# The sums of squares of q and k one head at a time, and the first S5 input products one tile later, in a two-layer hybrid trunk

## The chip, the core and the metric

The kernel runs on one core of one Trainium2 chip. The metric is the device time of one execution in microseconds (us): the median of three runs. Where time inside an execution is spoken of, it is counted from the first instruction of one profiled execution. PE is TensorE, DVE is VectorE, ACT is ScalarE, POOL is GpSimd, and SP is the engine that issues the transfers.

## What is computed

Two layers. Each is a SwiGLU block (1024 to 2 x 2816 and back, half a step), a mixing of the tokens, and a second SwiGLU block. A sequence is 16 learned tokens and 256 given ones, 272 in all. In the mixing one input projection feeds four groups of 512 channels, and one output projection takes their results back:

```
A: RG-LRU       conv over 4 tokens, h = a*h + b, times a GeLU gate
B: DeltaNet     q, k, v = silu(conv4(u)); q, k divided by their norms, sqrt(sum(x*x)+eps), per head
                S = S*exp(g) + k (beta*(v - ...))^T, done in chunks; 4 heads of 128
C: Mamba-2      conv over 4 tokens, chunked scan with a decay per head
D: S5           x -> complex diagonal state (64 per 16 channels) -> y; gelu; a half GLU
```

The sums of squares that the change moves are those of group B's norms: for each of 4 heads of q and 4 of k, the sum over 128 channels for each token. The S5 input products are those that bring group D's channels to its complex state, in four parts.

## The kernel before

**Tiles and precision.** x lies in SBUF as two halves, `xh` and `xl`, whose sum is x. A weight tile of 128 x 1024 comes by a transfer into `raw` (three buffers) and is split in `ahead` into `hi` (L215, on ScalarE) and `lo` (L217, on VectorE), with four buffers each (`SPLITS`). One tile of the input projection is 24 matmuls (`mm3`, L232 to L234: hi times xh, hi times xl, lo times xh, for 8 blocks of channels) into a PSUM bank `g`; there are four such banks. All other products use four banks `m`. The split of a tile is asked for three tiles ahead, and waits until the tile that last used its `hi` and `lo` buffers has been multiplied.

**What follows a tile.** A tile of q, k, v or of C's convolved channels goes through `conv` (a scaled copy on ScalarE, L540 or L542, and three steps on VectorE, L545) and `silu2` (tanh on ScalarE, L551, and a product on VectorE, L552). Its `g` bank is free once L545 has read it.

**Sums of squares.** `b_sums` (steps `ks` and `qs` with the head's number) squares a head on GpSimd (L580) and sums over channels with three matmuls of one column each (L240, in `token_sums`), into one `m` bank that is held from the first head of k until `b_norms` (step `bn`). A float matmul gives two records in the trace, so a head gives six.

**S5.** `d_in` (step `di`, part 0 to 3) is 8 small matmuls (L1179, 68 columns), four products on VectorE (L1184), two sums on GpSimd (L1185), two scans (L1194), four products (L1184) and two sums on GpSimd into the state `dz` (L1185). `d_out` (step `do`) is 12 small matmuls: L1213 on the input, L1215 on `dz`. ScalarE then copies the result out and SP writes and re-reads it (L1219, L1221). There is one state, so a part must be through `d_out` before the next part writes it. Steps `da` (L1229 and a GeLU, L862 to L865, on VectorE and ScalarE) and `ds` (L1236, ScalarE: the rounded half `dU`) follow, and `dg` is the half GLU: two weight tiles, each of 2 x 12 matmuls on `dU`, which need the four channels' `dU` and two `g` banks.

**Tokens' scalars and decays.** `token_scalars` (step `tk`) transposes (L475) and runs some 40 small VectorE operations (L476 to L491). `decay` (steps `R`, `be`) fills rows on ScalarE (L501), sums them on PE into three `m` banks one after the other (L517; L519 to L521; L523 to L525) and takes the exponential of each on ScalarE (L528), which needs a table load.

**What sets the order.** `STEPS_TEXT` (L81) is a hand-written list of steps, the same for both layers; `mixing` walks it and issues each step's work. A scheduler then fixes, before anything runs, one order of instructions for each engine, from that list and from the dependences. On the chip each engine takes its instructions in that order. So a step that is moved in the list can change the order on every engine, and far behind the place.

```
81  STEPS_TEXT = '''
82  du0 du1 du2 du3 k0 di0 k1 sm k2 do0 tk ks1 R0 ks0 q0 q1 di1 q2 k3 cB0 do1 qs0 qs1 ks3 ks2 q3 di2 qs3 cz0 v0 v1 da0 qs2
```

Of the kernel before, what the change touches and what calls it, by code (L numbers as in the profile page):

```python
# [78 lines left out]
A3 = {'lx': 0, 'x16': 256, 'x16t': 512, 'xu': 512, 'xt': 768, 'dc': 1024, 'dtc16': 1216}  # L79

STEPS_TEXT = '''  # L81
du0 du1 du2 du3 k0 di0 k1 sm k2 do0 tk ks1 R0 ks0 q0 q1 di1 q2 k3 cB0 do1 qs0 qs1 ks3 ks2 q3 di2 qs3 cz0 v0 v1 da0 qs2
do2 v2 be0 di3 bn cC0 bg0 R1 v3 be1 da1 do3 bg1 bg2 cx0 da2 bg3 bv0 da3 cC1 bb bv1 ds0 cB1 bc bm0 cz1 cx1 ds1 cg0 cg1 ds2
ds3 bv2 dg0 ax0 bf00 dg1 bm1 ax1 dn0 bf01 bf02 cx2 bf03 cx3 dn1 ax2 cz2 bf10 bf04 bs00 bf11 bs01 xd0 am2 am1 bs02 ax3
am0 xd1 bs03 am3 bs04 bf12 S0 bf13 ce0 bf14 ag0 bs10 bs11 cz3 bs12 ac ag1 bs13 bs14 bz0 S1 bz1 as0 ag2 xd2 bt0 bz2 ag3
# [1429 lines left out]
```

## Time and profile before

| | |
|---|---|
| median of 3 runs | 1440.14 us (1433.5 to 1443.87) |
| the profiled execution | 1442.42 us, of which its span 1440.5 us |
| mean granted clock of PE | 0.969 |
| busy: PE, DVE, ACT, POOL | 97%, 72%, 49%, 14% of the span |
| mixing of layer 0, of layer 1 | about 237 to 500 us, about 952 to 1216 us |

The span is the time from the first to the last instruction of the profiled execution. Busy time is the time in which an engine has an instruction under way; PE's matmuls overlap, so a row with several of them merged shows the time from the first one's start to the last one's end. The granted clock is a share of 2.4 GHz; 0.50 is the lower of its two levels, 1.2 GHz. "<-" in a wait names the engine, the tile and the line that ended it.

### The profile page before, as it was taken

What the parts mean: (1) busy time and instruction counts of PE and PEld (TensorE: products, weight loads), DVE (VectorE), ACT (ScalarE), POOL (GpSimd) and SP (SyncE); (2) the same over time, 40 slices, a digit from 0 to 9 for tenths busy, and PEclk for the clock granted to TensorE, in tenths of its full rate; (3) what the DMA queues carried; (4) which work ended last, traced back from release to release, by engine and by line L of the source; (5) the groups of instructions that cost most, each with busy time, mean ns of one, the idle gap of its engine ahead of it and who ended that gap; (6) DMA issues with size and microseconds to landing.
All of it is one profiled execution on the core that took longest, in us unless ns stands there. A gap on an engine that the chain in (4) does not pass through costs nothing. (4 is left out here: it accounts for less than half of the span.)

```text
span 1440.5 us, 27604 instructions
## 1 busy us (share of the span) xinstructions
PE 1392.0 (97%) x10848; PEld 1353.8 (94%) x10848; DVE 1036.4 (72%) x1936; ACT 708.4 (49%) x1226; POOL 205.4 (14%) x235
## 2 busy tenths in 40 slices
PE   7999999998999999999999999999989899999997
PEld 7999998997998999999999999989989889999997
DVE  6998787978985468887656665669888746666653
ACT  6445444454675355554444444444555745544442
POOL 1000010322322320000100000103332223100011
PEclk9999999999997999999999999999999979999998
DMA  7568775654422256777555555556544213666662
GB/s 238 179 188 265 235 254 163 217 171 120 126 77 71 82 155 217 254 230 254 172 162 184 175 170 174 172 161 211 177 127 141 74 45 114 186 187 187 188 182 85
DMA packets 94025, 243.73 MB, mean 169 GB/s; under 512 B 29496, under 2 KB 39496, under 8 KB 93896
## 3 DMA queue, kind: packets, MB, share of 16 engines
q1 hardware_dynamic: 93896, 241.97, 54.2%
q8 instruction: 85, 1.39, 0.4%
q14 instruction: 44, 0.36, 0.1%
HBM read 222.16 MB, written 19.78 MB: 168 GB/s over the span
## 5 line engine op out<-in xcount | busy, mean ns | idle before, releaser
L215 ACT ACTIVATE hi<-raw 128x1024 fp32r<-128x1024 f32 (+1 forms) x382 | 403.3, 1056 | 532.2 <-PE g L233 302.0
L217 DVE TENSOR_TENSOR lo<-raw,hi 128x1024 fp32r<-128x1024 f32 (+1 forms) x382 | 470.2, 1231 | 215.6 <-ACT hi L215 213.9
L232 PE MATMUL g<-xh,hi 128*128 128x272 f32 (+1 forms) x2048 | 597.7, 293 | 12.2 <-ACT hi L215 8.7
L234 PE MATMUL g<-xh,lo 128*128 128x272 f32 (+1 forms) x2048 | 595.8, 292 | 0.8 <-DVE lo L217 0.8
L233 PE MATMUL g<-xl,hi 128*128 128x272 f32 (+1 forms) x2048 | 595.3, 291 | 0.3 <-DVE xl L317 0.3
L232 PEld LDWEIGHTS g<-xh,hi 128*128 128x128 f32 x2048 | 391.4, 191 | 14.7 <-ACT hi L215 8.6
L234 PEld LDWEIGHTS g<-xh,lo 128*128 128x128 f32 x2048 | 390.7, 191 | 2.6 <-DVE lo L217 1.1
L233 PEld LDWEIGHTS g<-xl,hi 128*128 128x128 f32 x2048 | 391.5, 191 | 1.5 <-DVE xl L317 0.6
L277 POOL TENSOR_TENSOR acc<-acc,r 128x272 f32<-128x272 f32 (+1 forms) x42 | 43.3, 1032 | 556.1 <-ACT r L276 555.4
L233 PE MATMUL g<-r,hi 128*128 128x272 f32 (+1 forms) x256 | 73.2, 286 | 0.0
L360 DVE TENSOR_TENSOR r<-r,g 128x272 f32<-128x272 f32 (+1 forms) x88 | 38.1, 432 | 37.5 <-PE g L234 36.0
L545 DVE SCALAR_TENSOR_TENSOR r<-g,small,r 128x269 f32<-128x269 f32 (+2 forms) x120 | 59.1, 493 | 2.0 <-ACT r L542 0.4
L234 PE MATMUL g<-ra,lo 128*128 128x272 f32 (+1 forms) x192 | 55.2, 287 | 0.0
L232 PE MATMUL g<-ra,hi 128*128 128x272 f32 (+1 forms) x192 | 55.1, 287 | 0.0
L233 PE MATMUL g<-rs,hi 128*128 128x272 f32 (+1 forms) x192 | 55.0, 286 | 0.0
L233 PE MATMUL g<-rz,hi 128*128 128x272 f32 (+1 forms) x192 | 55.0, 286 | 0.0
L234 PE MATMUL g<-rq,lo 128*128 128x272 f32 (+1 forms) x192 | 54.6, 287 | 0.0
L232 PE MATMUL g<-rq,hi 128*128 128x272 f32 (+1 forms) x192 | 53.5, 289 | 0.2
L358 DVE TENSOR_TENSOR r<-g,rstd 128x272 f32<-128x272 f32 (+1 forms) x88 | 38.3, 435 | 15.6 <-PE g L234 14.8
L233 PEld LDWEIGHTS g<-r,hi 128*128 128x128 f32 x256 | 48.1, 188 | 0.0
L232 PE MATMUL g<-dU,hi 128*128 128x272 f32 (+1 forms) x96 | 29.7, 309 | 9.8 <-DVE r L545 9.8
L359 ACT ACTIVATE r<-r 128x272 f32<-128x272 f32 (+1 forms) x88 | 36.5, 415 | 5.4 <-DVE r L358 4.2
(412 smaller groups left out, 2461.5 us busy)
## 6 DMA issues: line engine op xcount, KB each, us to landing
raw<-in_wgu_dram SPq DMA_DIRECT2D x176, 512.0 KB
raw<-in_wdn_dram SPq DMA_DIRECT2D x88, 512.0 KB
raw<-in_win_dram SPq DMA_DIRECT2D x80, 512.0 KB
raw<-in_wout_dram SPq DMA_DIRECT2D x32, 512.0 KB
s5a<-spill SPq DMA_DIRECT2D x8, 920.0 KB
s5b<-spill SPq DMA_DIRECT2D x8, 896.0 KB
spill<-s5a SPq DMA_DIRECT2D x8, 648.0 KB
spill<-rx SPq DMA_DIRECT2D x4, 640.0 KB
```

Source lines behind the costliest of these rows:

```text
L215: nc.scalar.activation(out=hi[:, 0:w], in_=raw[:, 0:w], func=AF.Copy)
L217: ins = nc.vector.tensor_tensor(out=lo[:, 0:w], in0=raw[:, 0:w], in1=hi[:, 0:w].bitcast(F32), op=ALU.subtract)
L232: nc.tensor.matmul(ps, lhsT=hi, rhs=xh, start=start, stop=False)
L233: nc.tensor.matmul(ps, lhsT=hi, rhs=xl, start=False, stop=False)
L234: nc.tensor.matmul(ps, lhsT=lo, rhs=xh, start=False, stop=stop)
L277: (eng or nc.gpsimd).tensor_tensor(out=acc, in0=acc, in1=t, op=ALU.add)
L358: nc.vector.tensor_tensor(out=t, in0=g[:, t0], in1=r, op=ALU.mult)
L359: nc.scalar.activation(out=si, in_=t, func=AF.Silu)
L360: nc.vector.tensor_tensor(out=a, in0=si, in1=u[:, t0], op=ALU.mult)
L545: nc.vector.scalar_tensor_tensor(out=dst[:, o:T], in0=ps[:, 0:T - o], scalar=taps[:, j:j + 1], in1=dst[:, o:T], op0=ALU.mult, op1=ALU.add)
```

## The change

Line 82 of the list is written in another order; nothing else is changed. No operation is added or taken away. The step `di0` comes behind `k1` and no longer ahead of it. The steps `ks0` to `ks3` and `qs0` to `qs3`, of which `qs0 qs1 ks3 ks2` stood together and `ks1` and `ks0` with only `R0` between, now stand one at a time between steps that multiply dense tiles. The other steps keep their order among themselves, and so do the weight tiles that are fetched. The same line serves both layers.

```diff
--- before.py
+++ after.py
@@ -79,7 +79,7 @@
 A3 = {'lx': 0, 'x16': 256, 'x16t': 512, 'xu': 512, 'xt': 768, 'dc': 1024, 'dtc16': 1216}
 
 STEPS_TEXT = '''
-du0 du1 du2 du3 k0 di0 k1 sm k2 do0 tk ks1 R0 ks0 q0 q1 di1 q2 k3 cB0 do1 qs0 qs1 ks3 ks2 q3 di2 qs3 cz0 v0 v1 da0 qs2
+du0 du1 du2 du3 k0 k1 di0 sm ks0 k2 do0 tk ks1 R0 q0 q1 di1 ks2 q2 qs0 k3 cB0 do1 qs1 q3 ks3 di2 cz0 qs2 v0 qs3 v1 da0
 do2 v2 be0 di3 bn cC0 bg0 R1 v3 be1 da1 do3 bg1 bg2 cx0 da2 bg3 bv0 da3 cC1 bb bv1 ds0 cB1 bc bm0 cz1 cx1 ds1 cg0 cg1 ds2
 ds3 bv2 dg0 ax0 bf00 dg1 bm1 ax1 dn0 bf01 bf02 cx2 bf03 cx3 dn1 ax2 cz2 bf10 bf04 bs00 bf11 bs01 xd0 am2 am1 bs02 ax3
 am0 xd1 bs03 am3 bs04 bf12 S0 bf13 ce0 bf14 ag0 bs10 bs11 cz3 bs12 ac ag1 bs13 bs14 bz0 S1 bz1 as0 ag2 xd2 bt0 bz2 ag3
```

The scheduler's orders differ as follows at three places of layer 0; layer 1 is alike but for what is said. A row is the line, the operation, the tile written and the tiles read (with the program's numbers), and the shape.

**ScalarE, ahead of the first GLU tile (`dg0`).** `hi658` is a half of `dg1`'s weights, `hi671` of the tile behind them; L864, L862 and L1236 are the last steps of S5's channels, L542 the convolution that frees a `g` bank. Before:

```order
L215 ACTIVATE hi671_4545<-raw652_4429 128x1024
L864 ACTIVATE r624_4241<-r623_4240 128x272
L862 ACTIVATE r630_4271<-r629_4269 128x272
L1236 ACTIVATE dU641_4333<-dp124_972 128x272
L864 ACTIVATE r631_4272<-r630_4271 128x272
L542 ACTIVATE r636_4308<-g632_4277,small_73 128x272
L1236 ACTIVATE dU641_4333<-dp124_972 128x272
```

After the change:

```order
L862 ACTIVATE r630_4271<-r629_4269 128x272
L1236 ACTIVATE dU641_4333<-dp124_972 128x272
L215 ACTIVATE hi658_4465<-raw644_4362 128x1024
L864 ACTIVATE r631_4272<-r630_4271 128x272
L542 ACTIVATE r636_4308<-g632_4277,small_73 128x272
L1236 ACTIVATE dU641_4333<-dp124_972 128x272
L215 ACTIVATE hi671_4545<-raw652_4429 128x1024
```

The split into `hi671` uses the buffer of `hi634`, whose tile is the last one multiplied before `dg0`. It stood ahead of two L864, one L862, L542 and two L1236; now it stands behind the last L1236. What stands ahead of the last L864, L542 and L1236 is the split into `hi658`, whose buffer was `hi618`'s, one tile earlier. On VectorE the other half of that split (L217) goes from ahead of S5's last L863 and L865 to behind the three L545 that follow them, ahead of the three L545 of the next tile. On PE one set of L803 to L805 (three short products of group C) stands behind the last tile, where in layer 0 it stood ahead of it.

**PE, at the first decay stage (`be0`).** Before:

```order
L521 MATMUL m_3956<-r_3395,onesr 128x2x16
L240 MATMUL m_3166<-ones,r_3764 128x1 x2
L240 MATMUL m_3166<-ones,r_3764 16x1
L1215 MATMUL m_3895<-dz_973,s5b_3727 128x68
L523 MATMUL m_3957<-r_3395,ugt 128x2x144
L523 MATMUL m_3957<-r_3396,ugt 128x2x144
L524 MATMUL m_3957<-r_3395,onesr 128x2x16
L525 MATMUL m_3957<-r_3395,ugt_2745 128x2x16
L1215 MATMUL m_3895<-dz_973,s5b_3727 128x68
```

After the change:

```order
L521 MATMUL m_3956<-r_3400,onesr 128x2x16
L523 MATMUL m_3957<-r_3400,ugt 128x2x144
L523 MATMUL m_3957<-r_3401,ugt 128x2x144
L524 MATMUL m_3957<-r_3400,onesr 128x2x16
L525 MATMUL m_3957<-r_3400,ugt_2745 128x2x16
L240 MATMUL m_3166<-ones,r_3798 128x1 x2
L240 MATMUL m_3166<-ones,r_3798 16x1
L1215 MATMUL m_3895<-dz_973,s5b_3727 128x68 x2
L1213 MATMUL m_3895<-dU_1793,s5b_3727 128x68
```

The sums of one head (L240) and the first product of `do2` (L1215) stood between L521 and L523. Now L523 comes at once behind L521, and the sums and L1215 behind L525; the sums of another head have moved to just ahead of L517. On ScalarE the first L528 and its table load come directly behind the split that precedes them, where two convolution steps (L551, L540) stood between. Layer 1 had more of `do2` between L521 and L523 than layer 0, and now has none either.

**VectorE, at the first S5 input (`di0`).** Before:

```order
L1184 TENSOR_TENSOR r429_3189<-m427_3179,s5a425_3175 128x272
L1184 TENSOR_TENSOR r430_3190<-m428_3184,s5a425_3175 128x272
L1184 TENSOR_TENSOR r431_3191<-m428_3184,s5a425_3175 128x272
L1184 TENSOR_TENSOR r432_3192<-m427_3179,s5a425_3175 128x272
L552 SCALAR_TENSOR_TENSOR rk421_3165<-r424_3172,r423_3167 128x272
L476 COPY tk_2756<-m459_3346 128x32
L1194 SCALAR_TENSOR_TENSOR r433_3199<-s5a425_3175,r429_3189 128x272
L477 COPY tk_2756<-m459_3346 48x16
L217 TENSOR_TENSOR lo467_3440<-raw446_3277,hi466_3439 128x1024
```

After the change:

```order
L552 SCALAR_TENSOR_TENSOR rk421_3165<-r424_3172,r423_3167 128x272
L545 SCALAR_TENSOR_TENSOR r429_3206<-g425_3175,small_73,r429_3206 128x269
L545 SCALAR_TENSOR_TENSOR r429_3206<-g425_3175,small_73,r429_3206 128x270
L545 SCALAR_TENSOR_TENSOR r429_3206<-g425_3175,small_73,r429_3206 128x271
L217 TENSOR_TENSOR lo467_3440<-raw446_3277,hi466_3439 128x1024
L1184 TENSOR_TENSOR r435_3228<-m433_3218,s5a431_3214 128x272
L1184 TENSOR_TENSOR r436_3229<-m434_3223,s5a431_3214 128x272
L1184 TENSOR_TENSOR r437_3230<-m434_3223,s5a431_3214 128x272
L1184 TENSOR_TENSOR r438_3231<-m433_3218,s5a431_3214 128x272
L552 SCALAR_TENSOR_TENSOR rk421_3165<-r430_3211,r429_3206 128x272
L217 TENSOR_TENSOR lo474_3480<-raw452_3316,hi473_3479 128x1024
```

The product L552 of head 0, the three L545 of head 1 and the split into `lo467` come ahead of S5's first four products, and the token scalars' first copy (L476), with its L475 on PE, comes 15 rows later. On PE itself the eight L1179 of `di0` keep their place, inside the tile behind `k0` and `k1`. The rest of `do0` comes one tile later on PE, the sums of one head (L240) ahead of it, and the eight L1179 of `di1` directly behind it, with no tile between. The last four L1184 of `di1` are at rows 538 to 541 of VectorE's order, where they were at rows 543 to 546.

**Further back.** Behind `dg1` the lists differ again by a few rows, as far as the end of each layer's mixing. One such place is VectorE's in layer 1, in DeltaNet's chain over the chunks: there L722 (a difference whose result PE's L686 multiplies) stood behind the last of four reciprocals L902 of group A's coefficients and two splits L217; now it stands behind the third, ahead of the fourth and of the splits, and the copy L709 that the chain needs earlier stands ahead of all four.

## Rows read from the trace of the kernel before

**Rows 1.** The page: busy time by engine; then, from its part 5, one group of instructions.
```profile
PE 1392.0 (97%) x10848; PEld 1353.8 (94%) x10848; DVE 1036.4 (72%) x1936; ACT 708.4 (49%) x1226; POOL 205.4 (14%) x235
...
L217 DVE TENSOR_TENSOR lo<-raw,hi 128x1024 fp32r<-128x1024 f32 (+1 forms) x382 | 470.2, 1231 | 215.6 <-ACT hi L215 213.9
```

**Rows 2.** Waits of PE, 237 to 365 us (layer 0): total us, times, longest.
```profile
PE g L232 <- DVE r L545: 6.0, 1, 6.0
...
PE m L1215 <- POOL dz L1185: 2.0, 3, 0.8
...
PE m L523 <- ACT E L528: 1.4, 1, 1.4
```

**Rows 3.** Waits of PE, 952 to 1080 us (layer 1).
```profile
PE g L232 <- DVE r L545: 3.9, 1, 3.9
...
PE m L1215 <- POOL dz L1185: 2.5, 3, 1.1
```

**Rows 4.** Stretches: length, busy us (instructions) by engine, granted clock, DMA share, GB/s.
```profile
261.00:269.00 8.00, 7.93 (x65) 7.93 (x66) 7.90 (x25) 3.33 (x7) 1.25 (x3) 1.00 0.91 318
272.50:276.00 3.50, 3.50 (x18) 3.50 (x18) 3.23 (x7) 1.38 (x2) 1.53 (x2) 0.56 0.63 171
299.00:303.00 4.00, 4.00 (x22) 4.00 (x21) 4.00 (x6) 0.00 (x0) 2.66 (x2) 0.57 0.56 152
309.00:314.00 5.00, 5.00 (x31) 5.00 (x31) 2.60 (x5) 2.96 (x11) 1.17 (x3) 0.66 0.60 196
356.50:362.00 5.50, 5.50 (x26) 5.42 (x27) 4.46 (x16) 2.38 (x6) 0.00 (x0) 0.60 0.01 3
992.70:999.50 6.80, 6.80 (x56) 6.79 (x55) 6.52 (x14) 2.81 (x4) 1.54 (x2) 1.00 0.65 173
1002.80:1010.00 7.20, 7.20 (x37) 7.20 (x37) 5.25 (x17) 4.85 (x14) 2.24 (x4) 0.54 0.86 294
1071.00:1077.00 6.00, 6.00 (x37) 5.51 (x37) 5.20 (x17) 3.35 (x9) 0.16 (x1) 0.73 0.02 6
```

**Rows 5.** Timeline of PE: start, us, line, tiles, matmul records merged.
```profile
269.22 1.30 PE L240 MATMUL m<-ones,r 128*128 128x1 f32 x12
...
297.01 2.02 PE L240 MATMUL m<-ones,r 128*128 128x1 f32 x18
...
989.65 1.30 PE L240 MATMUL m<-ones,r 128*128 128x1 f32 x12
```

**Rows 6.** Timeline of VectorE and of GpSimd at the second S5 input, layer 0.
```profile
279.57 2.06 DVE L1184 TENSOR_TENSOR r<-r,s5a 128x272 f32<-128x272 f32 x4
...
281.79 0.76 POOL L1185 TENSOR_TENSOR dz<-r,r 128x272 f32<-128x272 f32 x1 [0.47 <-DVE r L1184]
```

**Rows 7.** Timeline of ScalarE and of PE at the first decay stage, layer 0.
```profile
303.66 1.06 ACT L215 ACTIVATE hi<-raw 128x1024 fp32r<-128x1024 f32 x1 [5.77 <-PE g L233]
...
305.40 1.28 ACT L528 ACT_TABLE_LOAD   x1
...
307.13 0.54 PE L523 MATMUL m<-r,ugt 128*128 128x288 f32 x2 [1.37 <-ACT E L528]
```

**Rows 8.** Timeline of ScalarE, VectorE and PE before the first GLU tile, layer 0.
```profile
350.41 1.06 ACT L215 ACTIVATE hi<-raw 128x1024 fp32r<-128x1024 f32 x1 [1.50 <-PE g L233]
...
354.77 1.55 DVE L545 SCALAR_TENSOR_TENSOR r<-g,small,r 128x269 f32<-128x269 f32 x3
...
357.35 1.57 DVE L545 SCALAR_TENSOR_TENSOR r<-g,small,r 128x269 f32<-128x269 f32 x3
...
356.47 0.57 PE L232 MATMUL g<-dU,hi 128*128 128x272 f32 x1 [5.98 <-DVE r L545]
```

**Rows 9.** Waits of PE, 361 to 520 us (rest of the mixing, layer 0).
```profile
PE m L686 <- DVE rs L722: 1.3, 1, 1.3
```

**Rows 10.** Timeline of VectorE and of PE in the chunk chain, layer 1.
```profile
1142.40 0.68 DVE L722 TENSOR_TENSOR rs<-rs,m 128x512 f32<-128x512 f32 x1
...
1143.22 2.05 PE L686 MATMUL m<-rs,rk 128*128 128x128 f32 x8 [4.93 <-DVE E L816]
```

## The prediction

> **What bounds the kernel now.** I read the busy shares first, then PE's waits, then the granted clock of short stretches, then the timelines around those that cost most. PE is busy for 97% of the span, VectorE for 72% [rows 1], so time is won where PE waits, or where it runs at 1.2 instead of 2.4 GHz. In layer 0's first half of the mixing PE waits three times for something that this change moves: 6.0 us for the convolution that frees a bank ahead of `dg0`, 2.0 us for S5's state, 1.4 us for the exponential at `be0` [rows 2]. Layer 1 has 3.9 and 2.5 us of the first two and nothing of the third [rows 3]. Around these places PE has stretches at a mean clock of 0.54 to 0.73, which is part 1.2 GHz, part 2.4 [rows 4]. A stretch of length t at mean clock c costs t(1-c): 1.5 us at 272.5, 1.7 at 299, 1.7 at 309, 2.2 at 356.5, 3.3 at 1002.8, 1.6 at 1071. Where PE is dense and at 2.4 GHz, 56 matmuls take 6.80 us [rows 4], so a tile of 24 takes about 3.0 us.
>
> The same operations are done before and after; a head's sums keep their price, 12 records for 1.30 us, so 0.65 us a head [rows 5]. All gain or loss lies in waits, clock and order. I go through the places.
>
> **1. The first GLU tile, both layers: the largest term.** In layer 0 ScalarE takes the split at 350.41 as soon as the last tile ends, and only then S5's last steps; PE resumes at 356.47, 5.98 us idle [rows 8]. So 6.06 us run from the tile's end to PE: the split (1.06), two rounds of S5's last steps (to 354.77), the convolution (1.55). After, the split ahead of the last round waits for a tile that ended one earlier, at 350.4 - 3.0 = 347.4 on the old time scale. Behind it come one round and not two, so I take half of the 3.3 us between 351.47 and 354.77: ready at 347.4 + 1.06 + 1.65 + 1.55 = 351.7. PE meanwhile multiplies the last tile and the six short products now behind it (an estimate of 0.2 us each), until 351.6. The wait is gone but for some 0.1 us. What is late next is the second half of `dg0`: its bank needs the next three L545 (1.57 us at 357.35 [rows 8]), and a split on VectorE (1.23 us [rows 1]) now stands ahead of these. That is 351.7 + 1.23 + 0.4 + 1.57 = 354.9, where the first half (1.5 us) ends at 353.2: a new wait of 1.7 us. Before, idle time and half clock cost 5.98 + 2.2 = 8.2 us; after 1.8 us, if the clock holds: -6.4. It may fall behind the new wait; I take -5.5. In layer 1 the same: 3.9 + 1.6 = 5.5 us before, 1.8 after, -3.7; I take -3.3. At the least, where another release is late, each keeps its old cost: 0.
>
> **2. S5's state, `do1`, both layers.** VectorE is busy for 7.90 of the 8 us from 261 [rows 4], and PE's wait follows it: the last L1184 of `di1` end at 281.63, the second `dz` at 282.55 [rows 6]. After the change `di0` is later on VectorE: three L545 and a split come ahead of it. But `do0` is later on PE too, by a tile of 3.0 us, so I take PE's wait for `do0` as unchanged. The last L1184 of `di1` stand five rows earlier in VectorE's order, since more of the token scalars comes behind them. VectorE does 25 instructions in 7.90 us [rows 4], 0.32 each, so five rows make -1.6 in layer 0; in layer 1 about the same, -1.5, out of a wait of 2.5 us in all [rows 3]. The token scalars end later; `be0`, which needs them, comes some 20 us behind `do1` (282.5 to 303.7 [rows 6, 7]), so I cost that at nothing. The ends are 0 (VectorE waits elsewhere and ends as late) and -2.0, -2.5 (the whole waits).
>
> **3. The sums.** 18 records ran in one go at 297.01 [rows 5], and PE fell to 1.2 GHz behind them: 1.7 us. Taken apart they should not do this; but with the second S5 input there is a new run of short matmuls (`ks0`, `do0`, `di1`, over 5 us with no dense tile). What this costs: the 12 records at 269.22 with an S5 input behind them were followed by a clock of 0.56; the same 12 with the same input at 989.65 by a clock of 1.00 [rows 4, 5]. So one such run cost 1.5 us or nothing. Both that fall and the one that may follow the new run lie ahead of the wait for `do1`, which takes them up. I count -1.2 in layer 0, 0 in layer 1. The half clock behind layer 1's `do1` (3.3 us) may go with the shorter wait; I count none of it and keep it for the range.
>
> The Trainium skill ("TensorE: Matmul & The Clock Gate", section "Part 1: The HAM clock gate") has the chip watch PE's activity in a window that runs freely, not started by the kernel, so that the same work may or may not lower the clock. The two equal runs agree with it. By this rule the falls that I count as gone may come back by chance: the sum would be 1.2 us higher.
>
> **4. `be0`.** In layer 0 PE waited 1.37 us at 307.13; ScalarE's split ran 303.66 to 304.72 and the table load from 305.40 to 306.68 [rows 7]. With the load directly behind the split, L523 can start at 304.72 + 1.28 + 0.45 = 306.45 (0.45 is what lay between the load's end and L523), 0.7 us earlier. But the sums and a part of `do2` that filled some 1.0 us of this time now come behind, and other sums fill time ahead. Net -0.3. In layer 1 PE did not wait, since more of `do2` stood between. Now nothing does: from the end of L521, an estimated 1.0 us behind the tile's end, to 1.06 + 1.28 + 0.45 = 2.8 us behind it, PE is idle for 1.8 us: +1.8. The half clock at 309 [rows 4] stays in layer 0, and may be new in layer 1 (up to +1.7).
>
> **5. The chain over the chunks, layer 1.** PE waits 4.93 us until 1143.22 for L722, which runs at 1142.40 [rows 10]. After, L722 stands ahead of the fourth reciprocal and of two splits (1.23 us each), so it could come 4 us earlier or more, and PE would have no other reason to wait. But so far back more has moved than I can follow. Bounds: 0 and -4.9; I take -2.0. In layer 0 PE's only wait over 0.4 us behind `dg0` is 1.3 us [rows 9]: from `dg0` on PE itself sets the pace, and what is won before stays won.
>
> **The sum.** Layer 0: -5.5 - 1.6 - 1.2 - 0.3 = -8.6. Layer 1: -3.3 - 1.5 + 1.8 - 2.0 = -5.0. Together -13.6 from the profiled execution's own 1442.4 us: 1428.8, say **1429**. That execution was 2.3 us above the median of the runs, 1440.1; I don't take this off, as some of the terms will not come in full. A measurement of this kernel tells about 1%, 14.4 us, from no change.
>
> **Rivals.** (a) *All of it comes.* The `dg0` terms in full (-10.1), `do1` -1.6 and -2.0, the falls at 299 and 1002.8 (-5.0), the chain -4.9, `be0` +1.5: -22.1, 1420. For it: PE sets the pace behind `dg0`. Against: each step has a release that may be late next. Chance 0.2.
>
> (b) *The gains are eaten.* VectorE, nearly full from 261 on, carries the same work; if it is the bound up to `dg0`, the splits L217 become what PE waits for, and a shorter wait at one place is a longer one at the next. Then only half of the first term is left, some -4: 1438. Against it: VectorE has an idle share in the rest, 28% of the span. Chance 0.23.
>
> (c) *Slower.* The new wait at `be0` decides: 1.8 us of idle time in layer 1, and behind idle time with short products the clock falls, as at 309 (1.7 us); so +3.5 there, and +0.4 with the same fall in layer 0. The new run of short matmuls at `do1` adds 1.5 us in each layer where it is not taken up: +6.9. This wins if `dg0` gives nothing, as when the second half's bank comes as late as the first's did: 1449. It decides as soon as the `dg0` terms together give less than 7 us and the others nothing. Chance 0.06.
>
> (d) *It does not do what it says.* On PE the eight L1179 of `di0` stand where they stood; "a tile later" is true of VectorE's order alone, and the gain at `dg0` is a by-product of the scheduler's. If only the sums' spacing counts, -1.2: 1441. Chance 0.03.
>
> The forecast holds 0.48, spread over 1421 to 1436.
>
> **The numbers.** Predicted 1429. For 8 in 10 the range goes from 1417, 3 us below (a), to 1442, which takes in (b) and (d); (c) and the ends of the others are left out. Faster by over 1% means below 1425.7: (a) and a third of the forecast's own, 0.36. Slower by over 1% means above 1454.6: the upper part of (c), 0.03. Within 1%: 0.61.
>
> **What would show it.** In the changed profile: PE's wait ahead of `dg0` under 1 us in both layers, and one of 1 to 2 us in the middle of `dg0` (step 1); the last `dz` of `di1` in layer 0 about 2 us earlier, counted from the mixing's start (2); no stretch under 0.8 clock around 299 (3); L523's wait in layer 1 of about 1.8 us (4); the wait at L686 in layer 1 well below 4.9 us (5). The prediction is wrong if PE still waits over 4 us ahead of `dg0`, if waits for `lo` (L217) appear between `do1` and `dg0`, or if the time won at 360 is no longer there at the end of the mixing.

## The result: slower by 1.3%, where 0.8% faster was forecast

The changed kernel takes 1460.88 us (median of 4 runs, 1457.2 to 1464.58), beside 1439.14 for the kernel before in the same comparison. The ratio on record is 1.013, with a 95% interval of 1.0102 to 1.0158 (the two medians as they stand give 1.015). The profiled execution has a span of 1462.1 us, 21.6 more than before. The forecast was 1429, with a range of 1417 to 1442.

First, the page: the row of PE and the row of the granted clock (forty slices of the span, in tenths), after the change,

```profile
PE 1409.1 (96%) x10848; PEld 1369.6 (94%) x10848; DVE 1032.7 (71%) x1936; ACT 707.3 (48%) x1226; POOL 207.3 (14%) x235
...
PEclk9999999779997999999999999998799979999998
```

and the clock row of the kernel before:

```profile
PEclk9999999999997999999999999999999979999998
```

The same 10848 matmul records keep PE busy 17.1 us longer than before [rows 1]. New are the sevens in slices 8, 9 and 29 and the eight in 28: the time went into a slower clock. To divide the span I cut it into slices of 2 us. A slice loses its length times (1 - granted clock) to the clock, and its length less PE's busy time to idling; the remainder is "work".

| us | span | lost to the clock | PE idle | work | clock, layer 0: 262-375, 375-520 | clock, layer 1: 990-1110, 1110-1225 |
|---|---|---|---|---|---|---|
| before | 1440.5 | 44.9 | 48.5 | 1347.1 | 8.5, 10.2 | 5.1, 13.7 |
| after | 1462.1 | 63.5 | 53.0 | 1345.6 | 17.1, 11.9 | 13.7, 13.7 |
| difference | +21.6 | +18.6 | +4.5 | -1.5 | +8.5, +1.7 | +8.5, 0 |

So the clock explains 18.6 of the 21.6 us, and nearly all of it is lost between the first S5 steps and `dg0`, the stretch that the change reorders. Three stretches carry it. First the changed kernel (length, busy us and count of PE, PEld, DVE, ACT, POOL, clock, DMA share, GB/s):

```profile
266.00:282.00 16.00, 16.00 (x83) 15.97 (x84) 10.46 (x38) 3.60 (x8) 1.94 (x3) 0.57 0.55 191
310.00:330.00 20.00, 19.26 (x90) 18.30 (x90) 13.00 (x33) 9.76 (x26) 7.82 (x9) 0.57 0.45 147
1038.00:1056.00 18.00, 17.25 (x78) 16.50 (x78) 10.76 (x28) 7.97 (x22) 6.95 (x9) 0.53 0.48 154
```

and the same places before:

```profile
266.00:282.00 16.00, 14.99 (x109) 14.56 (x107) 14.87 (x38) 6.40 (x11) 2.57 (x4) 0.89 0.57 180
305.00:325.00 20.00, 18.63 (x136) 17.96 (x136) 13.72 (x30) 11.45 (x27) 4.81 (x7) 0.91 0.59 186
1028.00:1046.00 18.00, 18.00 (x135) 16.64 (x134) 15.77 (x37) 10.13 (x24) 9.12 (x11) 1.00 0.53 180
```

PE is busy in both, so the busy share hides the loss; the count of its instructions (83 where there were 109) and the clock (0.57 where it was 0.89) show it. VectorE does less in the first stretch than before, 10.46 us for 14.87: from 262 to 283 us it waits 3.6 us for a split on ScalarE (L215), which itself waits for PE.

The timeline of PE after the change, layer 0 (start, us, line, tiles, records merged, wait):

```profile
265.88 0.44 PE L1215 MATMUL m<-dz,s5b 128*128 128x68 f32 x2 [0.79 <-POOL dz L1185]
...
266.38 0.68 PE L1215 MATMUL m<-dz,s5b 128*128 128x68 f32 x4
266.85 0.64 PE L1213 MATMUL m<-dU,s5b 128*128 128x68 f32 x2
267.28 1.06 PE L1215 MATMUL m<-dz,s5b 128*128 128x68 f32 x4
...
269.41 3.62 PE L1179 MATMUL m<-dU,s5a 128*128 128x68 f32 x16
...
273.16 0.43 PE L233 MATMUL g<-xl,hi 128*128 128x272 f32 x1
...
275.43 0.99 PE L240 MATMUL m<-ones,r 128*128 128x1 f32 x6
...
280.13 0.43 PE L232 MATMUL g<-xh,hi 128*128 128x272 f32 x1
...
280.65 0.29 PE L232 MATMUL g<-xh,hi 128*128 128x272 f32 x1
...
310.74 0.55 PE L523 MATMUL m<-r,ugt 128*128 128x288 f32 x2 [1.07 <-ACT E L528]
...
311.76 1.15 PE L240 MATMUL m<-ones,r 128*128 128x1 f32 x6
...
316.99 1.06 PE L1215 MATMUL m<-dz,s5b 128*128 128x68 f32 x4
...
361.30 0.36 PE L232 MATMUL g<-dU,hi 128*128 128x272 f32 x1 [0.33 <-DVE r L545]
...
364.32 0.36 PE L232 MATMUL g<-dU,hi 128*128 128x272 f32 x1 [1.28 <-DVE r L545]
...
435.68 2.04 PE L686 MATMUL m<-rs,rk 128*128 128x128 f32 x8 [4.38 <-DVE E L816]
```

Read it from above. In `do0` four records of L1215 take 0.68 us at 266.38 and 1.06 from 267.28 on: the clock has fallen inside the run, behind a wait of 0.79. The sixteen records of L1179 of `di1` follow at half speed. Then come dense tiles without a gap but for one head's sums, and a dense matmul still has 0.43 us at 273.16 and at 280.13; at 280.65 it has 0.29. A head's sums, 0.65 us at 2.4 GHz [rows 5], take 0.99 and 1.15. At `be0` it is the same: the wait of 1.07, the sums and `do2` behind it at half speed. Then the step that I expected to pay: in front of `dg0` 0.33 and 1.28 us are left of 5.98 [rows 8]. And 70 us further a wait of 4.38 at L686, which was 1.3 [rows 9]. The waits of PE after the change, 300 to 375, 375 to 520, 1030 to 1110 and 1110 to 1230 us (total us, times, longest):

```profile
PE g L232 <- DVE r L545: 1.6, 2, 1.3
PE m L523 <- ACT E L528: 1.1, 1, 1.1
...
PE m L686 <- DVE E L816: 4.4, 1, 4.4
PE m L686 <- DVE rs L726: 0.7, 1, 0.7
...
PE g L232 <- DVE r L545: 1.7, 2, 1.4
PE m L523 <- ACT E L528: 1.1, 1, 1.1
PE m L1215 <- POOL dz L1185: 0.7, 1, 0.7
...
PE m L686 <- DVE rs L726: 4.5, 1, 4.5
PE g L232 <- DVE tok L251: 2.0, 1, 2.0
PE m L517 <- ACT r L501: 1.6, 1, 1.6
PE m L686 <- DVE E L816: 1.5, 1, 1.5
```

In layer 1 the waits of the last stretch were, before:

```profile
PE m L686 <- DVE E L816: 4.9, 1, 4.9
PE m L519 <- DVE E L816: 1.4, 1, 1.4
PE m L686 <- DVE rs L726: 0.2, 1, 0.2
```

`dg0` and the chain behind it together wait 7.5 us before (6.0 + 1.3 + 0.2) and 6.7 after in layer 0; in layer 1, with that chain's other waits (L519, L251, L517), 10.4 and 12.2. What `dg0` gave came back there.

### The profile page after: what moved, and what is told of

Read it like the earlier page. It is cut to its first block, busy times and chain, and to the rows that moved or that the text cites. A ratio compares the mean times of both kernels' runs of the same rounds, so it can differ in the third digit from the quotient of the medians.

```text
span 1462.1 us, 27602 instructions
## 1 busy us (share of the span) xinstructions
PE 1409.1 (96%) x10848; PEld 1369.6 (94%) x10848; DVE 1032.7 (71%) x1936; ACT 707.3 (48%) x1226; POOL 207.3 (14%) x235
## 3 DMA queue, kind: packets, MB, share of 16 engines
q8 instruction: 86, 1.41, 0.4%
## 5 line engine op out<-in xcount | busy, mean ns | idle before, releaser
L215 ACT ACTIVATE hi<-raw 128x1024 fp32r<-128x1024 f32 (+1 forms) x382 | 403.1, 1055 | 545.2 <-PE g L233 312.6
L217 DVE TENSOR_TENSOR lo<-raw,hi 128x1024 fp32r<-128x1024 f32 (+1 forms) x382 | 469.8, 1230 | 224.0 <-ACT hi L215 219.3
L545 DVE SCALAR_TENSOR_TENSOR r<-g,small,r 128x269 f32<-128x269 f32 (+2 forms) x120 | 59.0, 492 | 3.0 <-ACT r L540 1.9
L234 PE MATMUL g<-rq,lo 128*128 128x272 f32 (+1 forms) x192 | 54.6, 287 | 0.0
L551 ACT ACTIVATE r<-r 128x272 f32<-128x272 f32 x40 | 17.0, 425 | 46.7 <-DVE r L545 24.3
```

The source lines that it names most:

```text
L215: nc.scalar.activation(out=hi[:, 0:w], in_=raw[:, 0:w], func=AF.Copy)
L217: ins = nc.vector.tensor_tensor(out=lo[:, 0:w], in0=raw[:, 0:w], in1=hi[:, 0:w].bitcast(F32), op=ALU.subtract)
L234: nc.tensor.matmul(ps, lhsT=lo, rhs=xh, start=False, stop=stop)
L545: nc.vector.scalar_tensor_tensor(out=dst[:, o:T], in0=ps[:, 0:T - o], scalar=taps[:, j:j + 1], in1=dst[:, o:T], op0=ALU.mult, op1=ALU.add)
L551: nc.scalar.activation(out=t, in_=x, func=AF.Tanh, scale=0.5)
```

## The experiments

Each kernel ran beside the kernel before on its chip (1443.6 to 1445.2 us); the ratio is to that. "Clock" in the last column is the loss from 262 to 375 us and from 990 to 1110, worked out as above; before has 8.5 and 5.1. These columns are of one profiled execution. Every run's own span and mean clock are on record too, so "all runs" gives span times (1 - clock), median and range. For the kernel before it is 45 us (39 to 54, 17 runs on one chip). The diffs show only the part of a line that changes.

| kernel | us | ratio, 95% interval | profiled span | clock, idle, work | clock lost, all runs | clock 262-375, 990-1110 |
|---|---|---|---|---|---|---|
| `ks1` later | 1453.31 | 1.0063, 1.0033 to 1.0093 | 1451.3 | 59.7, 48.5, 1343.1 | 58 (51 to 61) | 17.1, 8.5 |
| sums alone | 1450.02 | 1.0049, 1.0027 to 1.0072 | 1442.8 | 36.7, 58.5, 1347.7 | 46 (36 to 54) | 5.1, 6.8 |
| `di0` alone | 1449.36 | 1.0033, 1.0002 to 1.0063 | 1440.8 | 40.9, 51.9, 1348.0 | 47 (40 to 54) | 10.2, 8.5 |
| no sums | 1457.63 | 1.0086, 1.0055 to 1.0117 | 1457.0 | 60.7, 62.3, 1334.0 | 60 (57 to 61) | 20.5, 15.4 |
| before, regrouped | 1449.75 | 1.0038, 1.0015 to 1.006 | 1443.6 | 44.4, 52.5, 1346.8 | 46 (40 to 58) | 6.8, 3.4 |
| change again | 1463.66 | 1.013, 1.0078 to 1.0182 | 1462.5 | 67.5, 51.5, 1343.4 | 63 (55 to 67) | 17.1, 15.4 |
| `di3` later | 1450.06 | 1.0046, 1.002 to 1.0072 | 1444.7 | 48.5, 50.0, 1346.3 | 54 (46 to 60) | 15.4, 6.8 |
| filled | 1455.71 | 1.0084, 1.0055 to 1.0112 | 1454.1 | 45.4, 54.6, 1354.1 | 45 (39 to 53) | 6.8, 5.1 |
| `di3` later, filled | 1455.38 | 1.0079, 1.0053 to 1.0104 | 1453.0 | 51.7, 52.4, 1348.9 | 54 (46 to 57) | 15.4, 6.8 |

**PE's patterns alone.** The kernel's work is left out. PE multiplies dense tiles, with runs of 3 sums and 23 short products between, and with sums between tiles of 12 and 24.

```diff
+            s.dense(96 + 5 * rep)
+            s.sums(3)
+            s.s5s(23)
+            s.dense(72)
```

> The kernel's work is left out; PE alone runs patterns of dense matmuls (272 columns) and short ones (3 sums of one column; 23 products of 68 columns), with nothing to wait for. Block 1, four times: 96 or more dense, then 3 sums and 23 products (about 5 us), then 72 dense. Block 2, four times: the same, but the 72 dense are cut by 3 sums after every 12. Block 3, four times: 6 sums and 8 products, then 72 dense. Block 4: 16 times 24 dense and 3 sums. Block 5: 16 times 12 dense and 3 sums. Theory A (the run of short products lowers the clock, and single heads' sums in the dense work behind it keep it low): block 1 falls to 1.2 GHz for some 3 to 5 us behind each run, block 2 for 10 us or more, block 3 for 0 to 3.5 us, blocks 4 and 5 do not fall. Theory B (single heads' sums among dense tiles lower the clock by themselves): blocks 4 and 5 show stretches at 1.2 GHz. Theory C (the clock is not what costs; it is waits): no stretch at 1.2 GHz in any block, since PE never waits.

The clock left 2.4 GHz once in the 490 us, for 1.7 us of loss, behind one of the four runs of 6 sums and 8 products (the slow stretch at the very end aside). Of theory A's falls only this one came, of theory B's none; theory C had forecast none. PE does not wait in any of its runs. The clock row of its page:

```profile
PEclk9999999999999999999999999999999999999997
```

**`ks1` behind `q2`,** the change otherwise kept.

```diff
-k2 do0 tk ks1 R0 q0 q1 di1 ks2 q2 qs0 k3
+k2 do0 tk R0 q0 q1 di1 ks2 q2 ks1 qs0 k3
```

> The changed kernel with one step moved: ks1 goes from ahead of R0 to behind q2, so that in layer 0 the tiles behind the run ks0, do0, di1 are 48 dense matmuls, where they were 11, the sums of one head, and 37. The order on PE ahead of that is the same; behind do1 it differs. Theory A: the run still lowers the clock from about 266 us, but it comes back 3 to 5 us earlier than at 280.2 us; do1's last wait, at 288.25 us before, ends 2 to 3 us earlier, and the total is 1450 to 1458 us, where the changed kernel has 1461. Theory B: about the same clock, 1458 to 1464. Theory C: 1461, plus or minus 2.

The time is in theory A's range, and the clock returns 3 us earlier. The sums are gone from the tile behind `di1`, and the first stretch costs 1.7 us less (5.1 for 6.8). But `do1`, its two waits (0.65 and 0.77 us), six sums and the next S5 input now stand close together further on, with 8.5 us lost at 287 to 305 us, while PE no longer waits at `be0` and the stretch there is gone. In layer 0 the loss moved.

**The sums alone; `di0` alone.** The two halves of the change.

```diff
-k0 k1 di0 sm ks0 k2
+k0 di0 k1 sm ks0 k2
```

> The sums alone: the eight steps of sums stand as in the changed kernel, di0 is back ahead of k1. In layer 0 PE's order still has the sums of one head, do0 and a part of di1 in one run, sums behind 14 and 34 dense matmuls, and be0 with a head's sums and do2 in one run. Theory A: both long stretches at 1.2 GHz stay in layer 0, total 1450 to 1462. If it is di0's move that costs: 1436 to 1444, like the kernel before. Theory C: 1440 to 1450 by whichever waits come.

```diff
-k0 di0 k1 sm k2 do0
+k0 k1 di0 sm k2 do0
```

> The input product alone: di0 behind k1 as in the changed kernel, the sums in the order of the kernel before. In layer 0 do0 is a run by itself (about 2.2 us) with 24 dense matmuls behind it, and the sums of three heads stand together ahead of do2's tile. Theory A: no stretch at 1.2 GHz of over 8 us in the first half of the mixing, total 1434 to 1446. If di0's move is what costs: 1455 to 1465. Theory C: 1440 to 1450.

Neither half costs what both do: 0.5% and 0.3% for 1.3%. Theory A missed both times: with the sums alone the long stretches are gone, and `di0` alone takes 1449 us where it had 1446 at most. Both profiled executions were the quickest of ten, so their clock columns show the best case; by the median of all runs the clock takes 46 and 47 us, little more than before. With the sums alone PE's order has `do0`, four of `di1`'s L1179, then 14 dense matmuls, and the clock is 1.00 from 262 to 282 us. With `di0` alone there are 24 dense matmuls between `do0` and `di1`. Of the kernels up to here only those with both moves have one run of `do0` and all of `di1`.

**The patterns with a wait.** As the first, with copies on VectorE inside each run, for PE to wait for.

```diff
+                s.s5s(2)
+                nc.vector.tensor_copy(out=s.h[:, 2, 0:272], in_=s.psm[:, 0:272])
...
+                s.s5s(2 if block == 0 else 21)
```

> The kernel's work is left out, as in the first run of patterns; now PE waits once, for copies on VectorE, inside each run of short matmuls. Four blocks, each six times, with 96 or more dense matmuls ahead. Block 0: 2 products of 68 columns, the wait, 2 products, 72 dense. Block 1: 3 sums, 2 products, the wait, 21 products, 72 dense. Block 2: the same with 3 more sums behind the first 12 of the dense. Block 3: as block 1 without sums. Theory A2 (what lowers the clock is a wait together with the short run around it; sums in the dense work behind keep it low): block 0 does not fall; blocks 1 and 2 fall in most of the six, by some 4 to 8 us each, and block 2 stays low 2 to 4 us longer than block 1; block 3 falls less often than block 1. Theory A (the short run is enough): the same as the run without waits, which fell once in 12. Theory C (the data or the other engines matter, not PE's pattern): no fall in any block.

24 runs, and no fall (the lower last digit is the end of the program). But the waits of PE show that only 17 of the 24 had one, and of 0.53 us, where the changed kernel waits 0.79 in `do0`:

```profile
PEclk9999999999999999999999999999999999999998
...
PE m L1381 <- DVE h L1404: 9.1, 17, 0.5
```

So PE's shapes with a wait of 0.53 us do not bring the fall about; a wait as long as the kernel's was not tried. Nor do these programs have the kernel's data: their dense matmuls all have one tile as weights, mostly ones.

**No sums.** The three matmuls of each head are left out, and a constant stands for their result.

```diff
-        s.token_sums(s.psn, t, n, i + (4 if kind == 'q' else 0), 8)
+        pass
```

> The changed kernel with the 24 short matmuls of the sums per layer left out (the bank is set to a constant instead; GpSimd's squares stay), so that its values are not the reference's. In layer 0 do0 and di1 still run together on PE, with the wait for the state inside, and 72 dense matmuls behind; be0 and do2 still run together. The sums themselves are worth about 5.2 us each layer at full clock (48 records, 0.11 us each). Theory A2: without sums the run at do0 falls for less than the 14 us of the changed kernel, the one at be0 less than 17: 10 us or more below the changed kernel beside the sums' own price, so 1435 to 1445. If the S5 run with its wait is enough: the stretches stay, 1448 to 1456. Theory C: 1450.

Without one L240 the clock still falls in the joined run of `do0` and `di1`, 5.1 us lost at 267 to 278. PE's timeline (the L1179 need the same 3.62 us as above; the wait in `do0` has grown to 1.87):

```profile
266.49 0.44 PE L1215 MATMUL m<-dz,s5b 128*128 128x68 f32 x2 [1.87 <-POOL dz L1185]
...
271.48 3.62 PE L1179 MATMUL m<-dU,s5a 128*128 128x68 f32 x16
```

The theory that the sums are needed for the fall is refuted; the time is 1.6 us over the range for the S5 run with its wait. That the wait plays no part is not shown: without the sums PE waits longer, here and at `be0` (1.35 and 1.62 us).

**The list before, other sums moved.** `ks1` ahead of `do1`, `qs0` ahead of `qs2`, `qs1` behind `do2`. `do0` and `di1` stay apart by 46 dense matmuls.

```diff
-tk ks1 R0 ks0 q0 q1 di1 q2 k3 cB0 do1 qs0 qs1 ks3
+tk R0 ks0 q0 q1 di1 q2 k3 cB0 ks1 do1 ks3
```

> The list of the kernel before with four sums moved (ks1 to ahead of do1, qs0 to ahead of qs2, qs1 to behind do2, ks3 and ks2 stay together); di0 stays ahead of k1. On ScalarE the split into the tile behind dg1 stands behind S5's last step in both layers, as in the changed kernel; do0 and di1 are not together on PE. So the gain at the first GLU tile without the run at do0. Theory A2: PE's idle time ahead of dg0 under 1 us in both layers, no stretch at 1.2 GHz of over 8 us ahead of it, total 1428 to 1440, or 4 to 14 us below the kernel before on this chip. If the gain there is eaten by the chain behind it: within 3 us of the kernel before. If regrouped sums cost by themselves: 5 us above it or more.

This one loses as much to the clock in all as before (44.4 us in the profile, 46 by the median of its runs), though not at the same places: at `do1`, behind waits of 3.70 and 1.36 us, stands one stretch of 13.7 us at 1.2 GHz, where the theory had none over 8. It has the gain at `dg0`, and yet it is 5.5 us slower than the kernel before beside it, with 4.0 us more idle time in the profile. That is the time forecast for sums that cost by themselves; the waits suggest another reason. They are, 330 to 390 and 390 to 460 us:

```profile
PE g L232 <- DVE r L545: 1.6, 2, 1.3
...
PE m L686 <- DVE E L816: 4.4, 1, 4.4
PE m L686 <- DVE rs L726: 0.7, 1, 0.7
```

So the wait at L686 comes back without the change's greater loss to the clock.

**The change again.**

> The changed kernel once more, unaltered, beside the kernel before on the same chip. Theory (the time is lost at 1.2 GHz behind the joined S5 steps and behind be0, and belongs to the order of the work): ratio 1.010 to 1.016, and the trace again shows stretches below 2.4 GHz of 5 us or more at 266 to 282 and at 310 to 330 us, and one at 1038 to 1056; lost to the clock 52 to 62 us in all (sum of 2 us slices times one less the clock; 59.6 in the first trace, 45.9 in the kernel before). Rival (these stretches came by chance in one execution): lost 38 to 50 us in this one, with one or two of the three stretches gone, and a ratio that differs from the first by more than its interval.

```profile
266.00:282.00 16.00, 16.00 (x84) 15.97 (x84) 10.24 (x36) 3.39 (x7) 1.58 (x3) 0.58 0.51 178
310.00:330.00 20.00, 19.95 (x96) 19.04 (x97) 13.12 (x31) 9.08 (x24) 7.82 (x9) 0.57 0.41 136
1038.00:1056.00 18.00, 17.49 (x79) 16.63 (x80) 10.86 (x29) 7.28 (x20) 6.25 (x8) 0.55 0.41 141
```

The three stretches are there again, and so is the ratio. Without the slow stretch at the very end of the program, which the expectation's 59.6 leaves out too, the loss is 63.1, a little over its bound. The slower clock belongs to the order, not to one execution: the mean clock of the eight runs of this order on record is 0.954 to 0.962, and that of the seventeen of the kernel before beside it 0.963 to 0.973. Of the twelve stretches of the first execution ahead of that end, eleven came again within 1 us of their start and one 2.5 us later; two were 3.4 us longer and one as much shorter, and one of 3.4 us at 1122.6 was new. The Trainium skill ("TensorE: Matmul & The Clock Gate", section "Part 1: The HAM clock gate") lets the chip watch PE's activity in a window that runs freely and does not start anew with the kernel, so that the place where the clock changes can vary from run to run. These two traces show little of that; the 36 to 54 us over the ten runs of the sums alone agree with it better.

**`di3` later.** `di3` behind `bn`, `cC0` and `bg0`.

```diff
-do2 v2 be0 di3 bn cC0 bg0 R1
+do2 v2 be0 bn cC0 bg0 di3 R1
```

> The changed kernel with the fourth S5 input (di3) moved behind bn, cC0 and bg0: on PE its eight L1179 come 24 dense matmuls behind do2's last product and not 9, and three sums stand between. Theory (short steps close behind be0 keep the clock at 1.2 GHz there): the stretch at 310 to 330 costs 2 to 5 us and not 8.5, the one in layer 1 at 1038 to 1056 the same, ratio 1.004 to 1.009. Rival (it is the wait at be0 and what stands at be0 itself): both stretches cost 7 to 10 us as before, ratio 1.010 to 1.016.

The time is where the theory put it, the stretches only in part. Layer 1's is gone (clock 1.00 from 1030 to 1060); layer 0's costs 6.8, for 8.5, where 2 to 5 was expected and the rival had 7 to 10. The clock returns earlier there, but PE still waits 1.07 us at `be0`, and `do2` behind it still runs at half speed. In layer 1 the order had also moved at `do0` and at `be0`, where PE no longer waits, so the edit is not clean there and the rival is not excluded.

**Filled.** Dense matmuls that nobody reads among the short steps, 40 in each layer (the parts added to three lines).

```diff
+ s.nc.tensor.matmul(s.psn[:, 240:512], lhsT=s.onesr, rhs=s.xh[:, i, 0:T], start=True, stop=True)
...
+ [nc.tensor.matmul(ps[:, 272:512], lhsT=s.onesr, rhs=s.xh[:, k, 0:240], start=True, stop=True) for k in range(2)]
...
+ nc.tensor.matmul(ps[:, 272:512], lhsT=s.onesr, rhs=s.xh[:, q, 0:240], start=True, stop=True)
```

> The changed kernel with dense matmuls added that nobody reads: one of 272 columns behind each head's sums, two of 240 columns behind each half of an S5 input's products, and one of 240 columns ahead of each L1213 of an S5 output, 40 in each layer, some 0.11 us each at 2.4 GHz (a tile's 56 matmuls of 272 columns take 6.80 us), so +9 us of work in all; the scheduler's order shifts with it. Theory (the clock falls because these steps are short products with little in them): half or more of the loss between do0 and dg0 goes, 15 us or more of the 28 us that layer 0 and 1 lose there beyond the kernel before, and the time is 1448 to 1458. Rival (short products are not the reason; what counts is the waiting on VectorE and GpSimd, or chance): the clock's loss stays within 5 us of the changed kernel's and the time is 1465 to 1475.

The same three stretches:

```profile
266.00:282.00 16.00, 15.73 (x132) 15.45 (x130) 15.79 (x49) 7.16 (x12) 3.46 (x5) 1.00 0.63 215
310.00:330.00 20.00, 20.00 (x141) 18.86 (x141) 16.41 (x39) 10.33 (x26) 7.40 (x11) 0.91 0.49 163
1038.00:1056.00 18.00, 18.00 (x133) 16.71 (x134) 14.29 (x32) 12.14 (x27) 6.97 (x8) 1.00 0.45 148
```

The clock is back at 1.00, 0.91 and 1.00, and PE does 132 instructions where it did 83. The kernel has 8.5 us more work than the changed one and is 8.0 us shorter in the span: 18.1 us less lost to the clock, 1.6 more idle. The time and the clock are the theory's. This is the strongest evidence that the clock is the price. But the scheduler also put 5 dense matmuls of a tile in among those of `do0` and 8 ahead of `di1`, and the waits of 0.79 us in `do0` and 1.07 at `be0` are gone; in layer 1 a wait of 6.45 us for GpSimd's squares (L580) is new. So filling, keeping apart and covering a wait aren't told from each other here.

**`di3` later, filled.** Ten such matmuls in each layer; in layer 0 no tile comes in between `do0` and `di1`.

```diff
+            if u in (1,): [nc.tensor.matmul(ps[:, 272:512], ...) for q in range(1)]
...
+            if u in (0, 2) and q < 4: nc.tensor.matmul(ps[:, 272:512], ...)
```

> The kernel with di3 later (the one before this) and ten dense matmuls of 240 columns in each layer that nobody reads: one ahead of each L1213 of do0 and of do2, one behind each half of di1's products. From the sums of head 0 of k to the end of di1's products, PE's order is otherwise that of the changed kernel, with no dense tile among the products. Theory (the clock falls because such a run holds only short products): the stretch at 264 to 280 us costs 1.7 us or nothing, where it cost 5.1 with di3 later and 6.8 as changed; with 2 us of work added the time is 1442 to 1449. Rival (in the filled kernel it was the dense tiles that had moved in among the products, or the wait that they covered, and this little filling does nothing): 5 to 7 us lost there, time 1450 to 1456.

The loss is between the two: 3.4 us at 268 to 274, where the theory had 1.7 at most and the rival 5. A wait of 0.68 us in `do0` has stayed. So a little filling helps a little; the rest of the recovery above belongs to more of it, to the tiles in between or to the covered waits. The time is the rival's. Beside the profile of `di3` later, this one has 3.2 us more lost to the clock, 2.6 us more work and 2.5 us more idle time: in layer 0 the wait at `dg0` is back and the one at L686 has shrunk, in layer 1 L686 waits 4.9 for 2.2. The waits, 330 to 390 and 390 to 460 us:

```profile
PE g L232 <- DVE r L545: 6.2, 1, 6.2
...
PE m L686 <- DVE rs L722: 1.3, 1, 1.3
```

**The two waits over all eleven executions.** In layer 0 the wait at `dg0` and the first at L686 are: before 6.0 and 1.3; `ks1` later 3.9 and 1.3; `di0` alone 6.3 and 1.3; no sums 7.3 and 1.3; `di3` later, filled 6.2 and 1.3. On the other side: the change 1.6 and 4.4, twice; regrouped 1.6 and 4.4; filled 2.3 and 4.4; `di3` later 2.9 and 4.4; sums alone 3.9 and 4.4. No kernel has both short. The wait at L686 is 1.3 or 4.4 and nothing between: the profile names L722 as what ends it in the five with 1.3 and L816 in the six with 4.4, so VectorE's order differs there. It does not follow from the wait at `dg0` alone, as the two kernels with 3.9 show.

**The joined run.** In layer 0, `do0` and all of `di1` follow each other without a dense tile in six executions. The stretch there costs 6.8 (the change, twice), 5.1 (`ks1` later, no sums, `di3` later) and 3.4 (filled a little). In the five with dense tiles between them it costs 1.7 (before), 3.4 (`di0` alone) and nothing (sums alone, regrouped, filled). In layer 1 only the change, twice, has the joined run: 3.4 and 5.1.

Another difference sorts the executions better: how long PE waits for `dz` inside `do0`. Layer 0 of the kernel before and of `di0` alone (start, us, wait):

```profile
261.07 0.44 PE L1215 MATMUL m<-dz,s5b 128*128 128x68 f32 x2 [0.44 <-POOL dz L1185]
...
265.39 0.44 PE L1215 MATMUL m<-dz,s5b 128*128 128x68 f32 x2 [1.37 <-POOL dz L1185]
```

In layer 0 seven executions wait there 0.68 us or more, and in all seven a stretch at 1.2 GHz begins within 2.1 us of the wait's end; `di0` alone is one of them, with nothing joined. The four others wait 0.44 us or not at all, and none begins there (the 1.7 us of the kernel before come 11 us later, behind the sums and `di1`). In layer 1 a stretch follows in three of the four with 0.79 us or more (within 3.2 us), and in none of the seven with less. At `be0`, in either layer, a stretch follows all ten waits of 1.07 us or more; of the twelve places with no such wait two have one too. It isn't the whole rule: `do1` of the kernel before waits 0.83 and 0.79 us in layer 0 and keeps 2.4 GHz. How long a stretch lasts goes with what follows. In layer 0, behind such waits in an S5 output or at `be0`, it lasts 3.4 to 10.2 us where 19 to 24 dense matmuls stand behind the S5 output, and 10.2 to 17.1 where the next short steps come after 11 dense ones or fewer (6.8 with the little filling). Every joined run on record has a wait of 0.68 us or more in it, so the runs do not show what the joining does without the wait.

No kernel tried beats the one before.

## Why the prediction was wrong

**Step 1, `dg0`: right at the place.** 0.33 + 1.28 us in layer 0, 0.33 + 1.37 in layer 1, where I had 0.1 + 1.7. The half clock behind it went too. I compared when PE starts the n-th matmul of a dense tile from 235 us on, before and after. The changed kernel is 13.9 us late at the 400th (behind `be0`), 10.5 at the 480th, and 3.6 at the 520th: `dg0` gave 6.9 us, more than the 5.5 I counted.

**Step 5, "what is won before stays won": failed.** At the 840th the delay is 2.3 us, at the 880th 9.1. Between lies L686: it waits 4.38 us, and PE runs at 1.2 GHz from 434.0 us on, for 6.8 us (3.4 lost). VectorE reaches L722 at 434.86, behind the reciprocals L902 and two splits as before, but 7.4 us later. The timeline of VectorE after the change, layer 0, and L722 before:

```profile
428.15 1.83 DVE L902 RECIPROCAL r<-s5a 128x272 f32<-128x272 f32 x1
...
434.86 0.67 DVE L722 TENSOR_TENSOR rs<-rs,m 128x512 f32<-128x512 f32 x1
...
427.42 0.67 DVE L722 TENSOR_TENSOR rs<-rs,m 128x512 f32<-128x512 f32 x1
```

My reading, which no run tests by itself, is that PE has used up, in the time it no longer idles at `dg0`, the dense tiles that covered this. I had called the 1.3 us of [rows 9] PE's only wait and taken PE as the bound, without asking what a PE that comes earlier would meet there. In layer 1 I hoped for -2.0 at L686 [rows 10]; its first wait came down to 1.5, and others of 4.5, 2.0 and 1.6 took its place. This is rival (b), at another place than it named.

**Step 3, the clock: the step that set the sign.** I saw the new run of `ks0`, `do0` and `di1`, priced it at "1.5 us or nothing" by the clock after two shorter runs [rows 4, 5], and let the wait for `do1` take it up, so that the sum has -1.2 us for the clock here. It costs 6.8 us in layer 0 and 3.4 in layer 1 (5.1 the second time), and nothing takes it up: VectorE, full before, had slack as soon as PE ran slower, and PE ended its last wait for `do1` 5.6 us later in layer 0 (288.25 us for 282.61). The fall at 299 did go, as forecast, but one of the same length came behind `do1` at 290.7.

**Step 2, `do1`: its waits shorter, but not earlier.** They came down from 1.62 to 1.01 us in layer 0 and from 2.03 to 1.41 in layer 1, less than the 1.6 and 1.5 that I had. The wait for `do0`, which I took as unchanged, rose from 0.44 to 0.79 us and from 0.47 to 0.79. It stands inside the joined run, ahead of the fall.

**Step 4, `be0`: the wait right, its wake not.** Layer 0 waits 1.07 us for 1.37, -0.3 as counted. Layer 1 waits 1.07 and 0.73 more for `dz`, the 1.8 I had. But I allowed 1.7 us of half clock behind it in layer 1; it was 8.5 in each layer, where before had 1.7 in layer 0 and none in layer 1. Before, 21 dense matmuls followed `do2` in layer 0; now 9 do, and then `di3` and a head's sums.

**The rivals.** The mechanism is (c)'s: new waits at `be0` and short products in a row, and half clock behind. I gave it 0.06, made it depend on `dg0` giving nothing, and sized it at +6.9. At 18.6 us of clock it wins although `dg0` gave all it promised. The mis-sized term is the price of one such stretch: taken as 1.5 to 1.7 us from the shortest that the trace showed, it came out at 3.4 to 8.5. The trace of before held longer ones, 10.2 us lost at 450 to 470, and I had not put them among the bounds.

What stays open is whether a run of short matmuls lowers the clock by itself or by the wait that stood in each one here. The same shapes with no wait, or with one of 0.53 us, lowered it once in 36 runs.

## What to carry to other kernels

Where a change puts groups of short matmuls next to each other, or lengthens a wait among them, bound the price by the longest half-clock stretch of the trace, not by the shortest; a wait further on takes it up only if the engine waited for does not itself wait for PE. When a long wait is removed, look along the same engine for the next place where it runs into the engine that it waited for: here 3.5 of 4.4 us came back 70 us later. Dividing a span into clock, idle and work (span less the two) shows in one row of a table which of them a change has moved.

## What the runs showed of the hardware

In the changed kernel PE stayed at 1.2 GHz through 7.6 us of dense matmuls that followed each other without a gap (272.79 to 280.36 us), interrupted only by one head's sums; in `ks1` later, without these sums, through 4.8 us. Of the twelve stretches of one order, eleven came at the same places in a second execution, to 1 us; yet the ten runs of another order lost 36 to 54 us to the clock. And a program with 24 such runs of short matmuls, 17 of them with a wait of 0.53 us, kept 2.4 GHz but for its end.
